# An encoder layer with attention and mLSTM heads: the dot products of the last eight modulation columns move from the way into the FFN to the mLSTM stage

## Chip, core and metric

The kernel runs on one core of a Trainium2 chip. The core has a matmul engine (PE, whose weight loads are counted apart as PEld), a vector engine (DVE), a scalar engine (ACT), a general engine (POOL) and a queue processor (SP), which here issues nearly all transfers between DRAM and the on-chip memory. Each engine works through its own instructions strictly in the order in which the program holds them; one that has to wait holds up all that stand behind it on that engine. This goes for SP too: a transfer that may not be issued yet holds back the transfers behind it. The metric is the device time of one execution in microseconds, lower is better, as the median of several runs.

## What is computed

One layer on 1024 tokens of width 1024, all in float32. A conditioning vector `c` is turned into six shift, scale and gate vectors (the modulation), and these steer two residual blocks:

```python
cond = jax.nn.silu(c)
mod = cond @ w_ada[l] + b_ada[l]
sh1, sc1, g1, sh2, sc2, g2 = jnp.split(mod, 6, axis=-1)
h = modulate(rms_norm(x, norm_mix_g[l]), sh1, sc1)
proj = h @ w_in[l]
...
y_attn = axial_gqa_attention(q_a, k_a, v_a, q_norm_g[l], k_norm_g[l], tables)
y_mem = bidirectional_mlstm(qk_m, v_m, o_m, gates, conv_w[l], conv_b[l], gate_b[l], mlstm_norm_g[l])
mix = jnp.concatenate([y_attn, y_mem], axis=-1) @ w_out[l]
x = x + g1[:, None, :] * mix
h = modulate(rms_norm(x, norm_ffn_g[l]), sh2, sc2)
ffn = (jax.nn.silu(h @ w_gate[l]) * (h @ w_up[l])) @ w_down[l]
x = x + g2[:, None, :] * ffn
return rms_norm(x, final_norm_g)
```

The modulation is a row of 6144 numbers, each the dot product of `silu(c)` with one column of `w_ada`. Held as 48 columns of 128 numbers, the last eight columns (40 to 47) are `g2`, the gate of the FFN. It is used only where the FFN's result is added to the residual, at the very end.

## The kernel before

Features lie on the 128 partitions and tokens along the free dimension, so a matrix of 1024 by 1024 is eight tiles of 128x1024, or sixteen halves of 128x512. Products of float32 are made from a high and a low part of each operand: three matmuls on PE for one product (`mm3`, lines 294 to 297, a "triple" below). ACT makes the high part of a weight (`whi`), POOL the low one (`wlo`).

**The order of instructions** is set by a planner that runs while the program is written out. A `Clock` keeps an expected time for every engine and every transfer and emits each instruction when its inputs are expected to be there. PE's work is a set of generators, the streams, of which the first that is ready goes on; `ck.need(flags)` moves the expected time on until the flags are set and emits, on the way, the pending work of the other engines, but nothing of a stream of PE. On the chip only the resulting order on each engine remains, and the waits.

**The stages.** (1) Norm, modulation columns 0 to 15, the start of the input projection; (2) attention, with more of the projection as filler for PE; (3) the mLSTM stage; (4) the way into the FFN; (5) gate and up products; (6) the down product and the final norm.

**The mLSTM stage (line 1922 on)** handles four heads, one after another, as four streams: `states` (transposes of k, lines 1675 and 1703, tiles `mk`, `wv`, `U`, `Cs`), `front` (scores, tiles `E`, `W`, `mq`), `back` (numerators, tiles `na`, `ni`, `num`) and `transposed`, which turns a half head's finished result `hs` (line 1848). `last` holds the steps from the numerators to `hs`, on DVE, POOL and ACT; there is one buffer each for `hs` and `so`, so the next half head can write `hs` only when PE has turned the former. PE's filler is first the rest of the input projection, `chunk_unit`: eight pieces `acct` per chunk, stored as `v_d` or `o_d` through `vstg`. When its last piece is done, the pool `big` and the projection's input are closed, the residual stream `x` is loaded into their place (16 transfers), and the filler becomes `out_unit`, the output projection: 12 matmuls into a tile `acc` (two buffers), which DVE adds to `x` with the gate `mod[:, 16 + f]`. Head 2's `mk` and `v` are loaded at about the same place.

**The way into the FFN (line 1958 on)** has the 16 output units of the mLSTM's half: DVE adds each to `x`, ACT squares it, DVE sums the squares (`ssq`), a matmul with ones (`ms`, line 1159) makes the mean square, ACT and DVE its root (`nv`, `ny`), and `norm2` scales all tiles of `x` by it and splits them (`h11*h`, `h11*l`) for the first FFN products.

**The modulation's later columns** are loaded in halves of 128x512 (`ada`, 256 KB each) by `ada_late`, 64 in all, two for each of the columns 16 to 47. One call issues at most one half, and only if the half `ahead` places earlier is expected to be done; DVE then multiplies it with `cond` and sums in the same instruction (SCALAR_TENSOR_TENSOR into `modacc`). Since the `ada` tiles are a ring of `ahead` buffers, SP may issue a half only when DVE has done with the one `ahead` before. In the kernel before, 48 halves run during the projection and the attention. The last 16 (the columns of `g2`) run on the way into the FFN, in a pool of their own with a ring of four, after `cond` has been loaded and put through silu a second time:

```python
adpool = tc.tile_pool(name="ad", bufs=1, side="right")
PP["ada"] = adpool.__enter__()
cond_ok = load_cond(PP["ada"])
ck.streams([un], stop=lambda: cond_ok.done and ada_late(64, 4))
while not summed:
    ck.need(*adas[-2:])
    ada_late(64, 4)
adpool.__exit__(None, None, None)
```

`ada_late` returns nothing, so the stop condition never holds: it only serves to call `ada_late` between two pieces of PE's work.

Of the kernel before, what the change touches and what calls it, by code (L numbers as in the profile page):

```python
# [18 lines left out]
DRAM = bass.MemoryType.DRAM  # L19
# [50 lines left out]
class Flag:  # L70
    """done: what sets it is emitted; t: when that is expected to end"""
# [12 lines left out]
class Engine:  # L84
    """An engine's instructions with their expected times."""
# [39 lines left out]
class Clock:  # L125
    """Emits instructions in the order of expected times (us), each engine's in the order in which they are ready."""
# [16 lines left out]
    def chain(self, delay, *steps, flag=None, bg=None):  # L143
        """Functions that follow one another. bg: the engine of each step; the step waits until that is idle."""
# [24 lines left out]
    def dma(self, nbytes, issue):  # L169
        """delay until a transfer that is issued now has arrived"""  # L170
        self.dma_q = max(self.dma_q, self.now) + issue
        self.dma_t = max(self.dma_t, self.dma_q + 0.65) + nbytes / 360e3
        return self.dma_t + DMA_LAT - self.now
# [6 lines left out]
    def need(self, *flags):  # L180
        """What sets the flags is emitted before what follows."""
        for f in flags:
            while not f.done:
                self.pop()
            self.until(f.t)
# [10 lines left out]
    def add_pe(self, dt):  # L196
        """work of the tensor engine that is not a stream's"""
        self.t += dt
# [6 lines left out]
    def streams(self, mains, fills=(), stop=None):  # L205
        """Runs streams, the first that is ready first, until the mains have ended or stop() holds."""
# [14 lines left out]
class Stream:  # L221
    """A part of the tensor engine's work: a generator that yields the flags that its next piece needs."""
# [15 lines left out]
def layer_kernel(ctx, tc, xT, c, w_ada, vecs, cons, rope, w_f, w_t0, w_t, w_o, w_gu, w_d, out):  # L238
# [8 lines left out]
    # ---------------------------------------------------------------- constants  # L247
# [23 lines left out]
    # DRAM scratch  # L271
# [39 lines left out]
    def psum_open(name, tags, bufs=1):  # L311
        """tags: name -> (tag, buffers)"""
# [7 lines left out]
    class slot:  # L320
        """what frees the next tile of a tag"""
# [26 lines left out]
    with tc.manual_schedule():  # L348
# [12 lines left out]
        def load_cond(pool):  # L361
            """silu of c, the same for all partitions"""
# [11 lines left out]
        # ---------------------------------------------------- weights in a ring of six pieces  # L374
# [46 lines left out]
        def raw(shape, src, flag, arrived):  # L421
            """a transfer into the ring of three; flag: it has been used; arrived(tile, delay)"""
# [10 lines left out]
        def split(p, delay, src, shape, *before, lo=None):  # L433
            """the parts of a piece"""
# [12 lines left out]
        def piece(i):  # L447
            """a piece; its transfer, where it has one of its own"""
# [11 lines left out]
        def load_piece():  # L460
            """the next piece, once there is room for it"""
# [17 lines left out]
        # ---------------------------------------------------- norm 1, modulation, first three tiles  # L479
# [13 lines left out]
        for k in range(KT):  # L493
            def sum_up(k=k):
                """adds a tile's squares"""
# [34 lines left out]
        def rstd_steps(ms, scale, tag, put, flag=None):  # L530
            """1/sqrt(scale*ms + eps), with one Newton step"""
# [25 lines left out]
        def h_steps(k):  # L557
            """the modulated norm of a tile and its parts"""
# [22 lines left out]
        def h_when(k):  # L581
            """starts a tile when its columns of the modulation are there"""
# [26 lines left out]
        # ---------------------------------------------------- q and k: gain, mean square, rotation  # L609
# [6 lines left out]
        def rope_steps(i, accs):  # L616
            """i: q tile 0..3, or 4 for k"""
# [77 lines left out]
        # ---------------------------------------------------- units of the projection  # L695
# [3 lines left out]
        def tile_mms(w0, last):  # L699
            """two halves of a tile of features; last(n, acc, flag) when half n is summed"""  # L700
# [26 lines left out]
        def conv_unit(i, w0):  # L727
# [19 lines left out]
            def silu():  # L747
                """2*silu(y) = y*(1 + tanh(y/2))"""
# [23 lines left out]
        def chunk_unit(ci, w0):  # L772
# [5 lines left out]
            for j in range(NJ):  # L778
                if ci == 3 and j >= 5 and OPL[0]:
                    load_y(0, 0)  # L780
# [28 lines left out]
        # ---------------------------------------------------- gate rows: fw heads at 0..3, bw heads at 32..35  # L809
        def gate_steps():  # L810
# [100 lines left out]
            def decay():  # L911
                # decay of a chunk: exp(rend + mprev), spread over all partitions
# [19 lines left out]
        def ada_late(last=48, ahead=2):  # L932
            """the next half of a column of the modulation that is not needed at once"""
# [11 lines left out]
        # ---------------------------------------------------- attention  # L945
# [16 lines left out]
        def scores():  # L962
            """scores and softmax of a tile of queries"""
# [30 lines left out]
        def turned():  # L994
            """weights transposed, four tiles of keys"""
# [43 lines left out]
        # ---------------------------------------------------- output projection of the attention  # L1039
# [64 lines left out]
        # ---------------------------------------------------- norms of x1 over all features  # L1104
# [7 lines left out]
        def new_x1(k, n, dt):  # L1112
            """a place of a half tile of the residual stream, for that or for a part of an operand"""
# [6 lines left out]
        def spill(n, k, flag):  # L1120
            """the residual stream to DRAM; its place on chip takes parts of the FFN's operands"""
# [7 lines left out]
        def root(ms, w, then):  # L1129
            """1/sqrt(ms/D + eps), with one Newton step"""  # L1130
# [11 lines left out]
        def square(n, k, flag, then):  # L1142
            """adds a tile's squares; after the last: the reciprocal root of the mean square, for then(n, root)"""
# [21 lines left out]
        # ---------------------------------------------------- FFN's input: quarters, and their sums (Winograd's form)  # L1165
# [51 lines left out]
        # ---------------------------------------------------- FFN, gate and up: seven products for a pair of tiles  # L1217
# [29 lines left out]
        def set_piece(e, p, i, m):  # L1247
            """an operand of a set: a quarter of the weights or a sum of quarters"""
# [812 lines left out]
```

## Time and profile before

| | |
|---|---|
| median of the runs | 1433.75 us |
| the three runs | 1430.2, 1433.75, 1435.06 us |
| span of the profiled execution | 1431.8 us (its own time is not listed apart from its span) |
| PE busy | 1310.1 us, 91% of the span |
| DVE, ACT, POOL busy | 1075.9, 660.6, 792.6 us |
| mLSTM stage: first transposes to the last chunk piece | 515 to 574 us |
| mLSTM heads 2 and 3 with output units | 575 to 667 us |
| the 16 last halves of `ada`: issue of the first, end of the last on DVE | 673.6 to 726.4 us |

Each row of a view gives a start, a length, the engine, the line of the program, the operation and the tiles (output<-inputs). Nearly all work of DVE, ACT and POOL has line 96, as one helper records it, so such rows are told apart by their tiles. In brackets stand the idle time of the engine ahead of the row and what ended it.

### The profile page before, as it was taken

The page shows a single profiled execution, that of the slowest core. Times are in us where ns is not written, and L with a number is a line of the kernel's source. Part 1 is how long each engine was busy: PE and PEld are TensorE (multiplying, and loading weights), DVE is VectorE, ACT ScalarE, POOL GpSimd, SP SyncE. Part 2 cuts the span into 40 slices and gives each one's busy share as a digit, 9 for nine tenths or more (in the row PEclk, how much of TensorE's full clock was granted, in tenths as well). Part 3 has the DMA queues.
Part 4 walks back from the last instruction along what each step waited for, and adds up shares of the span by engine and source line. Part 5 has one row for each costly group of instructions (what it writes and reads, how often), then busy time and mean ns, then how long its engine had stood idle before and what let it go on. Part 6 is the DMA issues. An engine that isn't in the chain of part 4 may idle for free.

```text
span 1431.8 us, 19550 instructions
## 1 busy us (share of the span) xinstructions
PE 1310.1 (91%) x6594; PEld 1075.7 (75%) x6602; DVE 1075.9 (75%) x1542; ACT 660.6 (46%) x1191; POOL 792.6 (55%) x624
## 2 busy tenths in 40 slices
PE   5789799999999999899877899999999999979997
PEld 2577677888878988777655688888888887757786
DVE  6947989987788836776899786766666654988676
ACT  5444326677666645454555333332333234433462
POOL 5555454444444336766557564554544444799942
PEclk9899899999999999999999999999999999999999
DMA  7446452322112144824742342232333159623324
GB/s 285 158 127 198 148 153 78 118 66 77 44 52 60 38 136 127 291 94 165 239 155 67 102 141 103 96 106 101 111 110 102 62 185 339 247 67 88 103 63 151
DMA packets 103172, 184.40 MB, mean 129 GB/s; under 512 B 11296, under 2 KB 32672, under 8 KB 103072
## 3 DMA queue, kind: packets, MB, share of 16 engines
q1 hardware_dynamic: 89968, 161.06, 35.2%
q10 hardware_dynamic: 13104, 22.10, 4.2%
q8 instruction: 52, 0.85, 0.3%
q14 instruction: 48, 0.39, 0.1%
HBM read 136.19 MB, written 43.25 MB: 125 GB/s over the span
## 4 chain that ended last, share of the span: by engine, by line
PE 55%; DVE 19%; issue 8%; DMA 7%; POOL 6%; ACT 3%; SPq 1%; DVEq 0%; POOLq 0%; ACTq 0%
PE acc L296 13%; PE acc L295 13%; PE acc L297 13%; POOL wlo L96 3%; DVE x L96 3%; DVE ada L96 3%; DVE sst L96 3%; PE av L1025 2%; DMA wst<-act_d 2%; PE T L1006 2%; DVE PT L96 2%; PE S L974 2%; DVE y L96 2%; PE acct L295 2%; PE acct L297 1%
## 5 line engine op out<-in xcount | busy, mean ns | idle before, releaser
L96 POOL TENSOR_TENSOR wlo<-wst,whi 128x512 fp32r<-128x512 f32 (+2 forms) x208 | 309.0, 1492 | 227.4 <-ACT whi L96 211.2
L96 ACT ACTIVATE whi<-wst 128x512 fp32r<-128x512 f32 (+2 forms) x219 | 131.9, 606 | 141.8 <-PE acc L297 22.4
L96 POOL TENSOR_SCALAR P<-P,sst 128x1024 f32<-128x1024 f32 x64 | 88.9, 1392 | 141.2 <-DVE sst L96 99.8
L296 PE MATMUL acc<-x,whi 128*128 128x512 f32 x352 | 139.6, 397 | 3.3 <-DVE x L96 3.3
L96 POOL TENSOR_TENSOR wlo<-wr,whi 128x512 fp32r<-128x512 f32 x60 | 83.5, 1392 | 78.3 <-ACT whi L96 74.9
L295 PE MATMUL acc<-hh,whi 128*128 128x512 f32 x224 | 97.8, 436 | 13.5 <-ACT hh L96 11.3
L297 PE MATMUL acc<-whi,wcl 128*128 128x512 f32 x244 | 98.1, 402 | 9.5 <-POOL wcl L96 9.5
L96 ACT ACTIVATE P<-S,sst,colq 128x1024 f32<-128x1024 f32 x64 | 77.3, 1207 | 52.2 <-DVE sst L96 47.8
L295 PE MATMUL acc<-whi,wch 128*128 128x512 f32 x244 | 96.8, 397 | 4.0 <-ACT wch L96 4.0
L296 PE MATMUL acc<-hl,whi 128*128 128x512 f32 x224 | 92.8, 414 | 8.2 <-POOL hl L96 4.5
L296 PE MATMUL acc<-wlo,wch 128*128 128x512 f32 x244 | 96.9, 397 | 1.1 <-POOL wlo L96 1.1
L297 PE MATMUL acc<-hh,wlo 128*128 128x512 f32 x224 | 91.5, 409 | 0.0
L96 DVE SCALAR_TENSOR_TENSOR ada<-ada,cond 128x512 f32<-128x512 f32 (+1 forms) x79 | 84.9, 1082 | 7.3 <-DMA ada<-in_w_ada_dram 7.2
L96 DVE TENSOR_TENSOR sg<-acc,sg 128x512 f32<-128x512 f32 x67 | 45.4, 687 | 59.3 <-PE acc L297 58.9
L96 ACT ACTIVATE PT<-T 128x512 fp32r<-128x512 f32 x128 | 71.4, 597 | 37.8 <-PE T L1006 37.1
L96 DVE TENSOR_TENSOR PT<-T,PT 128x512 fp32r<-128x512 f32 x128 | 82.8, 681 | 7.2 <-ACT PT L96 7.1
L96 ACT ACTIVATE whi<-wr 128x512 fp32r<-128x512 f32 x60 | 37.9, 632 | 106.1 <-DVE wr L96 49.6
L96 POOL TENSOR_TENSOR wlo<-s,whi 128x512 fp32r<-128x512 f32 x44 | 60.8, 1383 | 38.3 <-ACT whi L96 31.7
L295 PE MATMUL acct<-whi,hh 128*128 128x256 f32 (+1 forms) x256 | 79.3, 310 | 2.4 <-ACT xp L96 1.0
L296 PEld LDWEIGHTS acc<-x,whi 128*128 128x128 f32 x352 | 66.5, 189 | 19.2 <-DVE x L96 4.2
L96 DVE SCALAR_TENSOR_TENSOR x<-acc,mod,x 128x512 f32<-128x512 f32 (+1 forms) x92 | 62.7, 719 | 24.1 <-PE acc L297 24.1
L1006 PE MATMUL T<-con,P 128*128 128x128 f32 x512 | 70.2, 275 | 10.4 <-DVE PT L96 7.6
(457 smaller groups left out, 3875.1 us busy)
## 6 DMA issues: line engine op xcount, KB each, us to landing
wr<-in_w_gu_dram SPq DMA_DIRECT2D x66, 256.0 KB, 2.8
ada<-in_w_ada_dram SPq DMA_DIRECT2D x64, 256.0 KB, 3.6
wd<-in_w_d_dram SPq DMA_DIRECT2D x22, 512.0 KB, 7.0
wst<-in_w_gu_dram SPq DMA_DIRECT2D x34, 256.0 KB, 3.1
wst<-act_d SPq DMA_DIRECT2D x33, 256.0 KB, 4.1
ada<-in_w_ada_dram SPq DMA_DIRECT2D x16, 512.0 KB, 4.9
wst<-in_w_o_dram SPq DMA_DIRECT2D x32, 256.0 KB, 4.3
act_d<-sg ACTq DMA_DIRECT2D x31, 256.0 KB, 2.0
```

Of the source, the lines that this page charges most:

```text
L96: return fn(*args, **kw)
L295: nc.tensor.matmul(acc, w[0], x[0], start=first, stop=False)
L296: nc.tensor.matmul(acc, w[0], x[1], start=False, stop=False)
L297: nc.tensor.matmul(acc, w[1], x[0], start=False, stop=last)
L974: nc.tensor.matmul(sp[:, halves(n)], qs[:, j * P:(j + 1) * P], k2[g][m][:, halves(n)], start=m == 0, stop=m == 1)
L1006: nc.tensor.transpose(tp[:, k], Pt[q][:, (4 * b + k) * P:(4 * b + k + 1) * P], ident)
L1025: nc.tensor.matmul(av, va[:, k, h // 4], PT[it][m][:, k], start=(k, m) == (0, 0), stop=(k, m) == (NJ - 1, 1))
```

## The change

`chunk_unit` calls `ada_late(64)`, with the default ring of two, before each of its pieces once the mLSTM stage runs. `cond` is loaded and put through silu at the start of that stage, in the pool `big`, which also holds the `ada` ring. After the last chunk piece a loop brings in what is left and sums it, before `big` is closed; the extra pool and the loop on the way into the FFN are gone.

```diff
@@ chunk_unit
             for j in range(NJ):
+                if OPL[0]:
+                    ada_late(64)
                 if ci == 3 and j >= 5 and OPL[0]:
                     load_y(0, 0)
@@ start of the mLSTM stage
-        bp = big_open(3)
+        bp = PP["ada"] = big_open(3)
+        load_cond(bp)
...
         ck.streams(mem, [un], stop=lambda: un.wait is None and all(f.done for v in vo_ok for f in v))
+        while not summed:
+            ck.need(*adas[-2:])
+            ada_late(64)
         BIGP[0].__exit__(None, None, None)
@@ the way into the FFN
-        adpool = tc.tile_pool(name="ad", bufs=1, side="right")
-        PP["ada"] = adpool.__enter__()
-        cond_ok = load_cond(PP["ada"])
-        ck.streams([un], stop=lambda: cond_ok.done and ada_late(64, 4))
-        while not summed:
-            ck.need(*adas[-2:])
-            ada_late(64, 4)
-        adpool.__exit__(None, None, None)
+        ck.streams([un])
         opool.__exit__(None, None, None)
```

The rest of the diff removes comments.

How the instructions stand on the engines shows at three places. The first is SP at the end of the last chunk, before: `o_d<-vstg` stores the last chunk piece, `x_...<-in_xT` are loads of the residual stream, `mk` and `v_...` are head 2's operands.

```order
L300 DMA wst<-in_w_o_dram 128x512 x2
L300 DMA o_d_96<-vstg 128x256
L300 DMA x_5900<-in_xT_dram 128x512
L300 DMA mk<-mqk_d_91 128x1024
L300 DMA v_5906<-v_d_94 128x8x128
```

The same place of SP, now.

```order
L300 DMA o_d_96<-vstg 128x256
L300 DMA so<-o_d_95 128x4x128
L300 DMA ada<-in_w_ada_dram 128x512
L300 DMA ym_d_82<-ymt 128x512
L300 DMA wst<-in_w_o_dram 128x512
L300 DMA ada<-in_w_ada_dram 128x512 x6
L300 DMA mk<-mqk_d_91 128x1024
L300 DMA v_6002<-v_d_94 128x8x128
L300 DMA x_6015<-in_xT_dram 128x512
```

Nine halves have gone out beside the chunks. The tenth, a store of the mLSTM's result, a weight load and the last six halves now stand between the last store of a chunk and the loads of head 2 and of `x`.

The second place is DVE there, before: the rows around the first addition of an output unit to `x` (`x_5900`), among them the steps of head 1's second half (`dn` to `hs<-hs,ss`), and head 2's first `W` and `Cs`.

```order
L96 SCALAR_TENSOR_TENSOR x_5900<-acc,mod,x_5900 128x512
L96 SCALAR_TENSOR_TENSOR dn<-num 128x8
L96 TENSOR_TENSOR dn<-dn,cols 128x8
L96 RECIPROCAL dn<-dn 128x8
L96 TENSOR_TENSOR hs<-num,dn 128x512
L96 SCALAR_TENSOR_TENSOR x_5922<-acc,mod,x_5922 128x512
L96 TENSOR_TENSOR hs<-hs,hs_5931 128x512
L96 SCALAR_TENSOR_TENSOR W<-tr,W 128x256 x2
L96 TENSOR_REDUCE ss<-hs_5931 128x4
```

DVE now, from the same step of head 1 (`hs_5901` is its scratch tile, `x_6015` the first tile of `x`).

```order
L96 TENSOR_TENSOR hs<-num,dn 128x512
L96 TENSOR_TENSOR hs<-hs,hs_5901 128x512
L96 TENSOR_REDUCE ss<-hs_5901 128x4
L96 TENSOR_SCALAR ss<-ss 128x4
L96 SCALAR_TENSOR_TENSOR ada,modacc<-ada,cond 128x512
L96 TENSOR_TENSOR hs<-hs,ss 128x512
L96 SCALAR_TENSOR_TENSOR ada,modacc<-ada,cond 128x512 x6
L96 TENSOR_TENSOR mod<-modacc,vec 128x8
L96 TENSOR_TENSOR mod<-mod,modacc 128x8
L96 SCALAR_TENSOR_TENSOR x_6015<-acc,mod,x_6015 128x512
L96 SCALAR_TENSOR_TENSOR x_6022<-acc,mod,x_6022 128x512
L96 SCALAR_TENSOR_TENSOR W<-tr,W 128x256 x2
```

The additions to `x` and head 2's `W` no longer mix with head 1's steps: they stand behind all of these and behind the last halves. On PE, which waits for them, both half heads of head 1 are now turned right behind the last chunk piece (eight transposes `tr<-con,hs`), ahead of the output units, which before surrounded them; then come seven triples of output units, head 2's first `tr<-con,mk`, one more triple, and one that needs the first addition to `x`. On POOL the steps of head 1's second half (`hs`, `so`, `ss`, `hs` again) now stand behind or between four low parts of output weights (`wlo`).

The third place is DVE on the way into the FFN, before, from the end of the root on (`x_...<-x_...,ny` scales a tile of `x`).

```order
L96 SCALAR_TENSOR_TENSOR ny<-nv,ny 128x512
L96 TENSOR_TENSOR ssq<-ssq,sq 128x512
L96 SCALAR_TENSOR_TENSOR ada,modacc<-ada,cond 128x512
L96 TENSOR_TENSOR x_6037<-x_6037,ny 128x512
L96 SCALAR_TENSOR_TENSOR x_5944<-acc,mod,x_5944 128x512
L96 TENSOR_TENSOR x_6071<-x_6071,ny 128x512
L96 SCALAR_TENSOR_TENSOR ada,modacc<-ada,cond 128x512
L96 TENSOR_TENSOR x_6086<-x_6086,ny 128x512
L96 SCALAR_TENSOR_TENSOR ada,modacc<-ada,cond 128x512
```

The same place now (`x_6129` to `x_6222` are the tiles that were `x_6037` to `x_6136`).

```order
L96 SCALAR_TENSOR_TENSOR ny<-nv,ny 128x512
L96 TENSOR_TENSOR ssq<-ssq,sq 128x512
L96 TENSOR_TENSOR x_6129<-x_6129,ny 128x512
L96 SCALAR_TENSOR_TENSOR x_6030<-acc,mod,x_6030 128x512
L96 TENSOR_TENSOR x_6143<-x_6143,ny 128x512
L96 TENSOR_TENSOR x_6163<-x_6163,ny 128x512
L96 TENSOR_TENSOR x_6184<-x_6184,ny 128x512
```

The dot products are gone from between the scalings; the rest keeps its order.

## The prediction

> **What bounds the kernel now.** I read the busy times of stretches first, to see which engine fills which stage; then the waits of PE; then the rows around each place that the change touches. The columns of the first view are the stretch, its length, the busy time and count of PE, PEld, DVE, ACT and POOL, the granted TensorE clock, the busy share of the DMA engines, and GB/s.
>
> ```profile
> 535.00:555.00 20.00, 19.83 (x148) 18.63 (x148) 14.25 (x40) 12.28 (x36) 12.28 (x19) 1.00 0.42 126
> ...
> 575.00:601.50 26.50, 26.47 (x135) 21.41 (x134) 18.46 (x32) 14.46 (x37) 24.22 (x35) 1.00 0.97 336
> 601.50:620.00 18.50, 14.73 (x76) 12.87 (x79) 14.56 (x34) 7.53 (x21) 10.30 (x16) 0.91 0.40 131
> 620.00:640.00 20.00, 18.23 (x97) 14.59 (x96) 15.57 (x35) 10.00 (x28) 15.33 (x21) 1.00 0.22 73
> 640.00:660.00 20.00, 19.74 (x103) 16.36 (x103) 16.45 (x36) 9.35 (x23) 14.11 (x11) 1.00 0.42 138
> ...
> 691.00:735.00 44.00, 32.94 (x114) 24.07 (x113) 40.82 (x59) 23.19 (x38) 23.86 (x15) 0.85 0.62 197
> ```
>
> Beside the first heads (535 to 555) and with heads 2 and 3 (575 to 601.5, 640 to 660) PE is the bound: 19.83 of 20, 26.47 of 26.5, 19.74 of 20 us. On the way into the FFN it is DVE: 40.82 of 44 us, while PE stands for 11 us and runs at a mean clock of 0.85. So the change takes work from where DVE is the bound to where PE is, and there any new wait of PE is lost time.
>
> The waits of PE from 660 to 900 us (engine, waiting tile, what it waited for: us in all, times, longest) name three that DVE makes there:
>
> ```profile
> PE acc L296 <- DVE h113l L96: 4.7, 1, 4.7
> PE ms L1159 <- DVE ssq L96: 3.3, 1, 3.3
> PE acc L296 <- DVE h111l L96: 2.3, 1, 2.3
> ```
>
> **What is removed on the way into the FFN.** Sixteen dot products leave DVE. In two stretches, for the tile `ada` alone (busy time of DVE first):
>
> ```profile
> 691.00:703.00 12.00, 5.30 (x10) 0.00 (x0) 0.00 (x0) 0.72 0.71 238
> ...
> 703.00:728.50 25.50, 8.71 (x14) 0.00 (x0) 0.00 (x0) 1.00 0.52 156
> ```
>
> The first stretch matters little:
>
> ```profile
> 691.57 0.39 PE L297 MATMUL acc<-yah,wlo 128*128 128x512 f32 x1
> ...
> 692.85 0.74 DVE L96 SCALAR_TENSOR_TENSOR x<-acc,mod,x 128x512 f32<-128x512 f32 x1
> ```
>
> The last addition to `x` of the first eight units waited behind a dot product, from 692.0, when PE was done with the unit, to 692.85: 0.8 us of the 3.3 us wait goes. The other dot products there ran while DVE would have waited anyway, for ACT's square and for the root. The second stretch is a closed queue from `ny` to `h113l`:
>
> ```profile
> 703.32 0.69 DVE L96 SCALAR_TENSOR_TENSOR ny<-nv,ny 128x512 f32<-128x512 f32 x1
> ...
> 704.53 1.78 DVE L96 SCALAR_TENSOR_TENSOR ada<-ada,cond 128x512 f32<-128x512 f32 x1
> ...
> 725.01 1.34 DVE L96 SCALAR_TENSOR_TENSOR ada<-ada,cond 128x512 f32<-128x512 f32 x1
> ...
> 728.88 0.68 DVE L96 TENSOR_TENSOR h113l<-x,h113h 128x512 fp32r<-128x512 f32 x1
> ```
>
> Seven dot products, 704.53 the first and 725.01 the last, take 8.7 us (the row above). Without them and 0.8 us earlier, `h113l` starts at 728.9 - 8.7 - 0.8 = 719.4. PE comes to it after its output units. In the next rows it starts `h113h` at 724.53, after the 2.3 us wait for `h111l`, so without both it gets there at 724.5 - 2.3 - 0.8 = 721.4, and `h113l` is there at 720.1. Both waits go: 2.3 + 4.7 = 7.0 us.
>
> ```profile
> 724.30 0.39 PE L297 MATMUL acc<-h112h,wlo 128*128 128x512 f32 x1
> 724.53 0.40 PE L295 MATMUL acc<-h113h,whi 128*128 128x512 f32 x1
> 729.62 0.79 PE L296 MATMUL acc<-h113l,whi 128*128 128x512 f32 x1 [4.69 <-DVE h113l L96]
> 730.21 0.63 PE L297 MATMUL acc<-h113h,wlo 128*128 128x512 f32 x1
> ...
> 734.48 0.63 PE L295 MATMUL acc<-h113h,whi 128*128 128x512 f32 x1
> ```
>
> After that wait PE runs slower, 0.63 us a matmul where it was 0.40. From 730.21 to 734.48 are ten steps of 0.427 us, where full-speed rows (724.30, 724.53) are 0.23 apart: 1.9 us, with the first and the last about 2.5. **The gain is 7.0 + 0.8 + 2.5 = 10.3 us.** Its bounds: 7 us, if the slow clock stays; and 14.0 us, all the dot products after 691 (5.30 + 8.71), if DVE, which is full again later, passes on each of them:
>
> ```profile
> 780.00:790.00 10.00, 4.92 (x19) 3.41 (x19) 10.00 (x10) 3.35 (x7) 7.07 (x5) 0.99 0.41 128
> ...
> 739.36 0.69 DVE L96 TENSOR_SCALAR nv<-ms 128x512 f32<-128x512 f32 x1 [2.20 <-ACT ny L96]
> ```
>
> I take 10.3, since DVE waits 2.2 us for the second root ahead of 739.36, by which its queue is used up: what PE loses up to there is what can come back. The DMA traffic of the sixteen halves goes too (4 MB); no wait of PE there names a transfer.
>
> **What is added beside the first heads.** Ten halves of the sixteen run there, by the order in front. A dot product takes, by the rows of `ada` over the whole span (shortest, median, longest in ns, so the halves set the median):
>
> ```profile
> L96 DVE SCALAR_TENSOR_TENSOR ada<-ada,cond x79: 654/691/2877, 22.2 to 725.0; 128x512 f32<-128x512 f32 x64, 128x1024 f32<-128x1024 f32 x15
> ```
>
> Ten times 0.69 are 6.9 us, in a stretch where DVE is busy 14.25 of 20 us: there is room, but each stands in DVE's order ahead of a `Cs` or `num` that PE soon needs, and holds DVE if its transfer is late. Between nothing and 6.9 us I take 1.5, nearer to nothing, because PE holds chunk pieces between most of its waits there.
>
> At the start of the stage come a load of `cond`, its silu and two ACT table loads, one to silu's and one back to the exponential's:
>
> ```profile
> 673.88 1.28 ACT L96 ACT_TABLE_LOAD   x1
> ```
>
> The load of `cond` can go out while SP waits for the last store of the attention. The table load back stands ahead of head 0's first `W`. Between nothing and 2.6 us I take 1.0.
>
> **What is added behind the last chunk.** Six halves are left there, and nothing of PE's work was emitted between them. I count from T, the end of the last chunk piece. SP now issues, in this order: the last `o_d`, `so`, half ten, `ym_d`, a weight load, six halves, head 2's `mk` and `v`, `x`. The times from issue to landing:
>
> ```profile
> wr<-in_w_gu_dram SPq DMA_DIRECT2D x66, 256.0 KB, 2.8
> ada<-in_w_ada_dram SPq DMA_DIRECT2D x64, 256.0 KB, 3.6
> ...
> mk<-mqk_d SPq DMA_DIRECT2D x4, 512.0 KB, 4.5
> ```
>
> Two things hold PE. First, it has to turn head 1's second half before any output unit. That half's `hs` needs the single buffer that PE frees by turning the first half, at T + 0.6. From there POOL is the slow engine; its rows of before for the same work:
>
> ```profile
> 579.77 1.29 POOL L96 TENSOR_TENSOR wlo<-wst,whi 128x512 fp32r<-128x512 f32 x1
> 581.40 1.05 POOL L96 TENSOR_TENSOR hs<-num,dn 128x512 f32<-128x512 f32 x1 [0.34 <-DVE dn L96]
> ...
> 587.40 1.02 POOL L96 TENSOR_TENSOR ss<-ss,both 128x4 f32<-128x4 f32 x1
> ...
> 590.25 0.62 POOL L96 TENSOR_SCALAR so<-so 128x512 f32<-128x512 f32 x1
> ...
> 593.50 1.29 POOL L96 TENSOR_TENSOR hs<-hs,so 128x512 f32<-128x512 f32 x1
> ```
>
> Four `wlo` stand among them now: 4 x 1.29 + 1.05 + 0.62 + 1.02 + 1.29 = 9.1 us, from T + 1.1 (after ACT's `vstg` and `whi`) to T + 10.2. PE idles from T + 0.6 to there: 9.6 us. Then it turns the half and runs seven triples of 0.70 us (three steps of 0.23), to T + 15.7.
>
> Second, `mk`. Half ten is multiplied at T + 6.5, ahead of DVE's `hs<-hs,ss`. The ring has two buffers, so of the last six halves the second, fourth and sixth follow half ten, each 3.6 + 0.7 + 0.1 = 4.4 us after the one before: multiplied at 10.9, 15.3 and 19.7. SP may issue the sixth at T + 15.4 and `mk` at T + 15.8, which lands at T + 20.3. PE idles from 15.7 to 20.3: 4.6 us. Then it waits for the first addition to `x`, which stands behind the sixth half on DVE and whose transfer left two places behind `mk`: 1.0 us more. **The loss is 9.6 + 4.6 + 1.0 = 15.2 us**, since before PE had no idle time at all from 575 to 601.5; its own first `tr<-con,mk` came 7.9 us after the chunk's end, with `mk` issued right behind the last store:
>
> ```profile
> 573.93 0.28 PE L297 MATMUL acct<-whi,hl 128*128 128x256 f32 x1
> ...
> 574.97 0.33 SPq L300 DMA_DIRECT2D o_d<-vstg  x1
> 575.35 0.42 SPq L300 DMA_DIRECT2D x<-in_xT_dram  x1
> 575.82 0.45 SPq L300 DMA_DIRECT2D mk<-mqk_d  x1
> ...
> 582.10 0.38 PE L1675 MATMUL tr<-con,mk 128*128 128x128 f32 x2
> ```
>
> Below: if the weights don't stand in POOL's way and the halves land in 2.8 us (the row of `wr`, the same size), 11 us. Above: if they land in 4.7 us, the median (second number) of the halves on the way into the FFN, 19 us.
>
> ```profile
> DMA to landing us min/median/max: 2.5/4.7/7.1
> ```
>
> A rule of the Trainium skill speaks for the change: "DMA: Bandwidth & Descriptors", Rules for kernel authors, says to overlap a transfer with compute by issuing it early and waiting for it late, so that its fixed setup cost is hidden. By the rule none of the landings would count and the last six would cost nothing; by the rows six of the sixteen can't be issued early, because the ring holds two. What the rule gives is the first rival.
>
> **The sum.** 15.2 + 1.5 + 1.0 - 10.3 = +7.4 us on the span of 1431.8, so 1439.2. The median of the three runs stands 1.95 us above that span, which I keep: **1441.2 us**, 0.5% slower. (About 0.3%, 4.3 us, is what a measurement of this kernel can tell from no change.) From the bounds: loss 11 + 0 + 0 to 19 + 6.9 + 2.6, gain 14.0 to 7, so -3 to +21.5 us, 1430.8 to 1455.3.
>
> **Rivals.**
> - *The transfers are hidden.* The last six halves land while PE has the seven triples and head 1's turns, and head 2's loads are not late. For it: DVE and SP have room there, and the halves are only 1.5 MB. Against it: the six are two deep and stand ahead of `mk` on SP. Then only the start costs 1.0 us: 1433.75 - 10.3 + 1.0 = 1424.5. It decides once the loss is under 10.3 - 4.3 = 6 us. Chance 0.12.
> - *The stall is there but is made good.* PE waits for DVE in heads 2 and 3 as well (from 601.5 to 640 it is busy 33.0 of 38.5 us, by two stretches of the same view), and if head 2's chain then runs with less in its way, or the gain nears 14, the two cancel: 11 + 1.5 + 1.0 - 14.0 = -0.5, 1433.3. Chance 0.14.
> - *The first heads are slowed as well.* Each dot product beside them holds DVE for its transfer, and SP, waiting for a buffer, holds the loads of `mq`. With 6.9 in place of 1.5 and the loss at its upper end: 19 + 6.9 + 2.6 - 10.3 = 18.2, 1452. Chance 0.10.
>
> **How the numbers follow.** My forecast, slower by 4.3 to 16 us (1438 to 1450), has 0.64. Slower in all: 0.64 + 0.10 = 0.74; within 0.3%: 0.14; faster: 0.12. The range from 1431 to 1450 leaves out the first rival and most of the third, 0.2 together.
>
> **What would show it.** Right: a group `tr<-con,hs` of eight whose second half waits some 9 us for POOL's `hs`; a wait of some 5 us of `tr<-con,mk` for its transfer; six `ada` on DVE about 2 us apart with waits for DMA between them; `mk` issued some 16 us after the last `o_d`; and behind it the waits for `h111l` and `h113l` gone, with 7 to 14 us less from `ms` to the second `ms`. Wrong: `mk` on chip within 8 us of the last chunk piece, or the `h113l` wait still there for another reason, such as POOL's halves of the same split.

## The result, and the profile after

The changed kernel takes **1443.54 us** (median of 4 runs, 1442.86 to 1445.63), the kernel before 1432.85 (4 runs beside it, 1430.2 to 1435.06): ratio 1.0064, 95% interval 1.0041 to 1.0088. It is slower. The profiled run took 1442.86 us, its span 1441.1 us, 9.3 us more than before.

The waits of TensorE (PE) in the changed kernel from 500 to 900 us (engine, waiting tile, what it waited for: us in all, times, longest):

```profile
PE tr L1850 <- POOL hs L96: 11.9, 2, 11.4
PE ms L1161 <- DVE ssq L96: 6.4, 2, 5.6
...
PE acc L295 <- DVE x L96: 3.7, 2, 2.8
...
PE tr L1677 <- DMA mk<-mqk_d: 1.9, 1, 1.9
```

The waits for `h111l` and `h113l` are gone (the one for `ssq` has grown from 3.3 to 6.4 us, as PE now comes to the second one sooner), and three new ones stand there: for `hs`, `mk` and `x`. Where they lie, by PE's instructions in order of time (start, duration, what it is; in brackets the idle time before it and what ended it):

```profile
579.72 0.28 PE L297 MATMUL acct<-whi,hl 128*128 128x256 f32 x1
580.51 0.66 PE L1850 MATMUL tr<-con,hs 128*128 128x128 f32 x4 [0.51 <-POOL hs L96]
592.60 1.12 PE L1850 MATMUL tr<-con,hs 128*128 128x128 f32 x4 [11.43 <-POOL hs L96]
593.37 0.78 PE L295 MATMUL acc<-yah,whi 128*128 128x512 f32 x1
593.94 0.63 PE L296 MATMUL acc<-yal,whi 128*128 128x512 f32 x1
...
601.42 0.42 PE L1677 MATMUL tr<-con,mk 128*128 128x128 f32 x2 [1.90 <-DMA mk<-mqk_d]
...
605.34 0.80 PE L295 MATMUL acc<-yah,whi 128*128 128x512 f32 x1 [2.80 <-DVE x L96]
...
713.86 1.12 PE L1161 MATMUL ms<-ssq,ones 128*128 128x512 f32 x2 [0.80 <-DVE ssq L96]
745.12 2.08 PE L1161 MATMUL ms<-ssq,ones 128*128 128x512 f32 x2 [5.62 <-DVE ssq L96]
```

The last chunk piece ends at T = 580.0. Behind it PE stands for 0.51 + 11.43 + 1.90 + 2.80 = 16.6 us. SyncE's (SP's) DMA queue in the same stretch:

```profile
580.50 0.33 SPq L300 DMA_DIRECT2D o_d<-vstg  x1
...
582.91 13.87 SPq L300 DMA_DIRECT2D ada<-in_w_ada_dram  x6
596.82 0.42 SPq L300 DMA_DIRECT2D mk<-mqk_d  x1
```

Six halves hold SP for 13.87 us, since each waits for one of two buffers; `mk` goes out 16.3 us after the last `o_d`. Busy times by stretch, with the columns of the prediction's first view:

```profile
535.00:555.00 20.00, 20.00 (x150) 18.75 (x148) 15.51 (x46) 12.22 (x36) 11.15 (x15) 1.00 0.49 145
...
579.90:607.50 27.60, 10.96 (x41) 7.93 (x41) 14.73 (x26) 5.48 (x10) 14.20 (x21) 0.72 0.64 215
...
709.60:753.60 44.00, 37.58 (x149) 28.64 (x148) 37.52 (x40) 26.94 (x45) 26.37 (x18) 0.92 0.54 173
```

Beside the first heads PE is as full as before (20.00 of 20 us). Behind the last chunk it works 10.96 of 27.6 us at a mean clock of 0.72. On the way into the FFN (the third row stands as far ahead of and behind the first `ms` as 691 to 735 did before) it works 37.58 of 44 us where it worked 32.94, at 0.92 for 0.85. The kernel before had its sums of squares at

```profile
695.26 2.08 PE L1159 MATMUL ms<-ssq,ones 128*128 128x512 f32 x2 [3.30 <-DVE ssq L96]
...
737.58 1.02 PE L1159 MATMUL ms<-ssq,ones 128*128 128x512 f32 x2
```

so 42.3 us lay between them, and 31.3 lie there now: 11.1 us are won. The first one comes 18.6 us later than before, though.

### The profile page after: what moved, and what is told of

Its sections match the earlier page's. It is cut to its first block, busy times and chain, and to the rows that moved or that the text cites. A ratio compares the mean times of both kernels' runs of the same rounds, so it can differ in the third digit from the quotient of the medians.

```text
span 1441.1 us, 19548 instructions
## 1 busy us (share of the span) xinstructions
PE 1310.1 (91%) x6602; PEld 1078.2 (75%) x6602; DVE 1083.1 (75%) x1542; ACT 661.0 (46%) x1192; POOL 792.0 (55%) x624
## 4 chain that ended last, share of the span: by engine, by line
PE 52%; DVE 21%; issue 7%; POOL 7%; DMA 7%; ACT 5%; SPq 1%; ACTq 0%; DVEq 0%; POOLq 0%
PE acc L296 12%; PE acc L295 12%; PE acc L297 12%; DVE x L96 4%; DVE ada L96 3%; POOL wlo L96 3%; PE av L1027 2%; DVE sst L96 2%; PE T L1008 2%; DVE y L96 2%; PE S L976 2%; DVE PT L96 2%; DMA qd<-q_d 2%; PE acct L295 1%; PE acct L297 1%
## 5 line engine op out<-in xcount | busy, mean ns | idle before, releaser
L96 POOL TENSOR_TENSOR wlo<-wst,whi 128x512 fp32r<-128x512 f32 (+2 forms) x208 | 304.0, 1467 | 219.9 <-ACT whi L96 206.3
L295 PE MATMUL acc<-hh,whi 128*128 128x512 f32 x224 | 97.3, 435 | 13.4 <-ACT hh L96 11.1
L96 DVE SCALAR_TENSOR_TENSOR ada<-ada,cond 128x512 f32<-128x512 f32 (+1 forms) x79 | 80.4, 1025 | 22.8 <-DMA ada<-in_w_ada_dram 22.5
L296 PEld LDWEIGHTS acc<-x,whi 128*128 128x128 f32 x352 | 66.6, 189 | 16.7 <-DVE x L96 1.6
```

The lines of the kernel that those rows point to most:

```text
L96: return fn(*args, **kw)
L295: nc.tensor.matmul(acc, w[0], x[0], start=first, stop=False)
L296: nc.tensor.matmul(acc, w[0], x[1], start=False, stop=False)
```

## The experiments

Kernels that were timed together ran on one chip and shared the runs of the kernel before, so each row has the median of before beside it; rows with different medians of before are compared by their ratios. The last column is read from each trace: from the end of the last chunk piece (the last `acct` row) to the start of the first `ms`. The change has no part in that stretch but its halves and what they shift. (For the kernel before it is 121.1 us, but there, as in e1, some 2.6 us of head 1's products run behind the last chunk that the other kernels run ahead of it.) It is from one execution each, and those of e3 and e9 took 4.5 and 5.5 us longer than their medians. The runs that leave dot products out also set `modacc` to zero at the start.

| run | dot products | us (before) | ratio, 95% | chunk end to `ms` |
|---|---|---|---|---|
| e1 | none | 1424.06 (1435.41) | 0.9908, 0.9883–0.9933 | 121.6 |
| e2 | 9 beside chunks | 1426.14 (1435.41) | 0.9929, 0.9909–0.9950 | 117.0 |
| e3 | 9, stretch without PE work | 1433.50 (1435.41) | 0.9985, 0.9970–1.0001 | 125.4 |
| e4 | 9 + 7 beside heads 2, 3 | 1438.33 (1435.41) | 1.0019, 1.0004–1.0034 | 127.8 |
| e5 | 9 + 7 behind the store, no transfers | 1436.88 (1435.16) | 1.0013, 0.9999–1.0027 | 127.2 |
| e6 | e3, low parts on DVE | 1434.38 (1435.16) | 0.9993, 0.9978–1.0008 | 124.4 |
| e7 | change, `mk`, `v` ahead of the 7 | 1440.60 (1435.16) | 1.0046, 1.0029–1.0064 | 130.5 |
| e8 | 16 beside chunks, ring of four | **1427.01** (1435.16) | 0.9952, 0.9933–0.9971 | 118.1 |
| e9 | e3, units ahead of the turn | 1437.58 (1433.23) | 1.0027, 1.0008–1.0046 | 127.9 |
| e10 | change, units ahead of the turn | 1447.73 (1433.23) | 1.0090, 1.0067–1.0112 | 138.7 |
| e11 | 9 + 7 on the way into the FFN | 1431.60 (1433.23) | 0.9985, 0.9967–1.0003 | 117.6 |
| e12 | e4 without its 7 | 1435.19 (1434.98) | 0.9996, 0.9978–1.0014 | 126.6 |
| change | 9 + 7 behind the store | 1443.54 (1432.85) | 1.0064, 1.0041–1.0088 | 133.9 |

**e1, e2: the gain alone, and the nine beside the chunks.**

```diff
 e2:     bp = PP["ada"] = big_open(3)
         load_cond(bp)
 ...
-        while not summed:
-            ck.need(*adas[-2:])
-            ada_late(64)
+        mod_sum(40, 48)
 e1, besides: no call of ada_late(64) in chunk_unit, no load_cond(bp)
```

> The change without the last sixteen dot products at all: neither the nine beside the chunks, nor the seven behind the last store, nor the second load of the condition (the modulation's columns 40 to 47 are left out and hold only their bias). What is left is the gain on the way into the FFN. Theory: the time before less 10.3 to 11.2 us (the working's gain, and what the changed trace shows between the two sums of squares), 1421.5 to 1422.5 us. Rival, by which the new way into the FFN is bound by something other than the dot products (POOL's halves of the split, the square roots): less than 6 us come back, 1427 or more.

> The change with the nine halves beside the last chunks and the load of the condition, but without the seven behind the last store (those seven dot products are left out). Theory: the nine cost little, 2.5 us (the working's 1.5 for the first heads and 1.0 for the start) to 3.2 us (by how much the last chunk piece ends later in the changed trace, less the head 1 work that now stands ahead of it) above the run without any, 1424 to 1426 us. Rival, by which the first heads carry the loss: each of the nine holds DVE for its transfer, 7 us or more above the run without any, over 1429, and the seven add little.

Without any dot product the kernel is 11.4 us faster by the medians (13 by the ratio); with the nine 9.3 us. So the gain is there, and the nine with the load of the condition cost some 2 us of it, which the intervals don't tell from nothing. In the run with nine hardly anything holds PE behind the last chunk (0.5 us for `hs`, and behind `mk` 1.6 us for `x`):

```profile
579.83 0.28 PE L298 MATMUL acct<-whi,hl 128*128 128x256 f32 x1
...
588.39 0.38 PE L1678 MATMUL tr<-con,mk 128*128 128x128 f32 x2
...
697.12 1.13 PE L1162 MATMUL ms<-ssq,ones 128*128 128x512 f32 x2 [0.48 <-DVE ssq L96]
```

Its `mk` is turned 8.3 us after the chunk's end (before: 7.9). So the loss is with the last seven.

**e3: the planner's stretch without the seven.** While the loop runs, the planner's clock moves on 30.2 us and nothing of PE's streams is written out.

```diff
-        while not summed:
-            ck.need(*adas[-2:])
-            ada_late(64)
+        ck.until(ck.t + 30.2)
+        mod_sum(40, 48)
```

> The change with the nine halves, and in place of the seven only the planner's stretch of 30.2 us in which nothing of TensorE's work is written out (the seven dot products are left out, and their transfers too). It keeps the order in which the engines get head 1's end, and takes the transfers from SP and the dot products from DVE. Theory (two causes, the order on POOL and the transfers on SP): PE still waits 9 to 12 us for POOL's hs in head 1's second half, but no longer for mk and x; of the 18 us between the run with nine and the changed kernel, about half comes: 1432 to 1436 us. Rival A, all of it is the order: 1441 to 1444. Rival B, all of it is the transfers in front of mk: 1424 to 1427, with no wait for hs over 3 us.

```profile
595.14 1.12 PE L1851 MATMUL tr<-con,hs 128*128 128x128 f32 x4 [10.76 <-POOL hs L96]
...
602.49 0.38 PE L1678 MATMUL tr<-con,mk 128*128 128x128 f32 x2
```

The theory's number came: 7.4 us above e2, with the wait for `hs` whole and those for `mk` and `x` gone. The changed kernel, 1.0064 x 1435.41 = 1444.6 on this chip, stands another 11 us above (8.5 by the last column). Two causes, neither of them small.

**e6, e9: what in the stretch costs.** First the weights' low parts are taken from POOL:

```diff
-                (lo or gps).tensor_sub(p[1], src(), p[0].bitcast(F32))
+                (lo or LO[0] or gps).tensor_sub(p[1], src(), p[0].bitcast(F32))
 ...
+        LO[0] = dve
         ck.until(ck.t + 30.2)
+        LO[0] = None
```

> The run with the stretch alone (the seven dot products left out), with the low parts of the four output weights that are written out in that stretch made by DVE in place of POOL. Theory (the working's first term: POOL's queue is what PE waits for): 4 x 1.26 = 5 us of POOL's work go, the wait for hs falls from 10.8 to 5 to 7 us, and the time from 1433.5 to 1427 to 1430. Rival: the wait is the chain of head 1's end itself (DVE, ACT and POOL in turn), with the weights in POOL's own idle time: the wait stays at 9 us or more and the time over 1431.5.

The theory fell. The wait went from 10.76 to 9.41 us, and the time not at all. DVE, ACT and POOL in that run:

```profile
585.12 0.68 DVE L96 TENSOR_TENSOR hs<-hs,hs 128x512 f32<-128x512 f32 x1
...
588.59 0.63 ACT L96 ACTIVATE whi<-wst 128x512 fp32r<-128x512 f32 x1 [1.61 <-DMA wst<-in_w_o_dram]
589.25 0.69 DVE L96 TENSOR_TENSOR wlo<-wst,whi 128x512 fp32r<-128x512 f32 x1 [1.47 <-ACT whi L96]
589.86 0.68 DVE L96 TENSOR_TENSOR hs<-hs,ss 128x512 f32<-128x512 f32 x1
...
590.69 1.26 POOL L96 TENSOR_TENSOR hs<-hs,so 128x512 f32<-128x512 f32 x1 [1.81 <-DVE mod L96]
```

With no weight left on POOL, POOL waits (1.81 us) for DVE, and DVE waited for a weight whose transfer was late. So the run doesn't take the weights out of the chain's way altogether: on DVE the low parts at 582.45, 584.51 and 589.25 put its next steps off by 0.4, 0.6 and 0.7 us. Estimated from these rows, the chain without any weights would still hold PE for some 8 of the 10.8 us. Head 1's end is a chain over DVE, POOL and ACT that is long by itself. In the kernel before it took longer still, from this row to POOL's last `hs` (593.50 to 594.79, in the prediction's rows), 15 us, and PE was busy all along:

```profile
579.73 0.16 DVE L96 SCALAR_TENSOR_TENSOR dn<-num 128x8 f32<-128x8 f32 x1
```

What the stretch takes away is PE's work beside the chain. So the next run gives it some, 9 us of output units ahead of the second turn:

```diff
+        t0 = ck.t
+        ck.streams([un], stop=lambda: ck.t > t0 + 9.0)
         ck.streams(mem, [un])
```

> The run with the stretch alone (1433.5 us; the seven dot products left out), with 9 us of the output units written out ahead of the second turn of head 1. The engines' work for head 1's end is the same. The run with the low parts on DVE took the weights out of POOL's queue and PE still waited 9.4 us for hs, so that head 1's end is slow by itself, and what is missing is work for PE beside it. Theory: with fourteen triples (0.70 us each, 9.8 us) between the two turns the wait for hs falls under 3 us and the time to 1425 to 1429, near the run with nine (1426.1). Rival: the units that are put there are missing as cover beside heads 2 and 3, which then wait as much longer: 1431 or more.

The rival held. PE's waits from 500 to 900 us:

```profile
PE acc L296 <- ACT yah L96: 6.5, 1, 6.5
PE acc L296 <- DVE x L96: 5.8, 2, 4.9
...
PE tr L1851 <- POOL hs L96: 2.2, 2, 1.6
```

The wait for `hs` is nearly gone, one for `x` comes at once (4.85 us, ahead of 593.88), and one for `yah` behind the last turn of head 3 (ahead of 680.88), where the units are now missing. The time became 4 to 6 us worse than e3's (by the medians and by the ratios). Head 2's first `mk` is turned 8.3 us after the chunk's end in e2, 19.3 in e3 and 26.3 in e9. That this later start is what the stretch costs fits these rows, but no run shows it by itself; moving units about changes the name of the wait and doesn't bring the time back.

**e5, e7, e10: the seven transfers.** First the seven dot products without their transfers (each takes again the half that is on chip), then the two loads of head 2 ahead of the seven, then the units of e9 in the changed kernel itself.

```diff
 e5:
+            if n >= 57:
+                t, arrive = still[0], ck.dma(P * HALF * 4, 0.5)
 e7:
+        ck.need(*heads[0]["back"])
+        load_head(2)
         while not summed:
 ...
-            load_head(h)
+            if h != 2:
+                load_head(h)
```

> The changed kernel, but the last seven dot products run again on the half that is on chip already, so that their seven transfers (1.75 MB) are left out (seven sums come out other than they should); the planner's stretch and the seven instructions on DVE stay. The run with the stretch alone took 1433.5 us, and the changed kernel would take 1444.6 on that chip by its ratio of 1.0064. Theory: of those 11 us nearly all are the transfers, that is mk, v and x behind them on SP and the dot products waiting for them; seven dot products that wait for nothing are 4.9 us on a DVE that is idle there: 1432 to 1437 us, mk issued within 7 us of the last o_d, no wait for x over 1 us. Rival: it is DVE's time, with head 1's end and the additions to x behind the dot products: 1440 or more.

> The changed kernel, all sixteen dot products, but mk and v of head 2 are issued ahead of the seven halves (as before the change, right behind the last store) instead of behind them. Theory: the place of these two loads on SP is half or more of the 11 us between the stretch alone (1433.5) and the changed kernel (1444.6 on that chip): 1435 to 1439.5 us, no wait of PE for mk. Rival: the seven dot products themselves, with the first additions to x behind them, carry it: 1441 or more, and PE waits for x 4 us or more where it waited for mk.

> The changed kernel, all sixteen dot products, with the same 9 us of output units ahead of the second turn of head 1. Theory: the order alone doesn't mend it, since the units need their additions to x, and these stand on DVE behind the seven dot products with their transfers; there are two accumulators, so after two units (5.6 us) PE waits for x instead of hs, 8 us or more: 1438 to 1445. Rival: the wait for hs was most of the loss, and PE gets over it here: 1434 or less.

Without the transfers (e5) 3.4 us are left above e3 (4 by the ratios), hardly more than the intervals, so the transfers carry some 7 of the 11; the wait for `hs` is the same 11.43 us as in the changed kernel. With `mk` and `v` first (e7) PE waits for neither, and the time comes down only by about 4 us (1444.3 by the ratio on that chip, to 1440.6): a third of the 11 where half or more was expected, and just above the range. PE still waits 9.71 us for `hs`, and the wait for `mk` has moved to the next thing behind the seven. In e7, PE and DVE:

```profile
601.08 1.23 PE L1785 MATMUL na<-v,W 128*128 128x130 f32 x4 [4.38 <-DVE W L96]
...
599.71 0.69 DVE L96 SCALAR_TENSOR_TENSOR ada<-ada,cond 128x512 f32<-128x512 f32 x1 [1.13 <-DMA ada<-in_w_ada_dram]
...
600.61 0.75 DVE L96 SCALAR_TENSOR_TENSOR W<-tr,W 128x256 f32<-128x256 f32 x2
```

What PE gives to this `W` (`tr<-mq,mk`, started at 592.76, 1.05 us) was done at 593.8; it stands behind the last dot product on DVE, which waits for its half. With the units ahead (e10) the mechanism is the expected one, larger than I put it (1447.73 for at most 1445): two units run, then PE stands 15 us for the addition behind the seven:

```profile
602.26 0.77 PE L295 MATMUL acc<-yah,whi 128*128 128x512 f32 x1 [14.98 <-DVE x L96]
```

**e4, e12, e11, e8: other places for the seven.**

```diff
 e4, after the x loads of heads 2 and 3 (e12: the load alone):
+        adpool = tc.tile_pool(name="ad", bufs=1, side="right")
+        PP["ada"] = adpool.__enter__()
+        cond_ok = load_cond(PP["ada"])
-        ck.streams(mem, [un])
+        ck.streams(mem, [un], stop=lambda: cond_ok.done and ada_late(64, 1))
 e11: no loop; the pool "ad", load_cond and ada_late(64, 4) of before on the way into the FFN
 e8:
-                    ada_late(64)
+                    ada_late(64, 4)
+                    ada_late(64, 4)
 ...
-            ada_late(64)
+            ada_late(64, 4)
```

> All sixteen dot products: nine beside the last chunks as in the change, and the other seven beside heads 2 and 3, one at a time, with a load of the condition of their own, and no stretch without TensorE's work. Theory: what costs is where the seven stand, not that they run; one half of 0.7 us every 5 us or more fits on DVE beside heads 2 and 3, so 0 to 4 us above the run with nine, 1424 to 1430, faster than both kernels. Rival: heads 2 and 3 have no room either (PE busy there 19.7 of 20 us in places), and each of the seven delays PE by its 0.7 us and its transfer: 1433 or more.

> The run with nine halves beside the chunks and, at the start of heads 2 and 3, the load of the condition and its silu, but none of the seven dot products there (they are left out). The run with both (seven dot products one at a time beside heads 2 and 3) came out at 1438.3 us where 1424 to 1430 was expected, the run with neither at 1426.1. Its trace shows head 2's first na about 4.5 us later against the last chunk piece, with PE waiting 2.4 us for ACT's silu and two table loads of 1.28 us, and 6.4 us more between there and the first sum of squares. Theory: the condition costs 4 to 6 us and the seven dot products the rest: 1430 to 1432. Rival A: all of it is the condition, whose place shifts the order behind it: 1436 or more. Rival B: all of it is the dot products: 1428 or less.

> All sixteen dot products: nine beside the last chunks as in the change, the other seven on the way into the FFN as before the change, four at a time, with a load of the condition there, and no planner's stretch. Theory: the gain of 11 us belongs to the dot products in the closed queue of DVE between the two sums of squares (seven of them ran there before); seven of sixteen go partly where DVE waits anyway, so 2 to 6 us of the gain are lost: 1428 to 1432 us, on or under the time before. Rival: any dot product there costs its share, or the load of the condition and its silu set the end: 1434 or more.

> All sixteen dot products beside the last chunks: a ring of four halves in place of two, and two halves asked for at each chunk piece, so that none is left for behind the last store. Theory: nine cost 2.1 us there (1426.1 against 1424.1), so sixteen cost 3.7: 1427.8 us (1425.5 to 1430.5), faster than both kernels, with no stall behind the last chunk beyond what the run with nine has. Rival: the room beside the first heads is used up by nine, and the seven more cost their 0.7 us and part of their landing each, 6 us or more above the run with nine: 1432 or more.

e4 missed: 12 us above e2. By e12, some 9 of them are the second load of the condition and some 3 the seven dot products (e4 and e12 have intervals that overlap), so e12 came out above its theory's range too, by 3 us, and close under the rival that gave all of it to the condition. ACT and PE in e12:

```profile
586.76 1.28 ACT L96 ACT_TABLE_LOAD   x1 [1.95 <-DMA cond<-in_c_dram]
588.05 1.06 ACT L96 ACTIVATE cond<-cond 128x1024 f32<-128x1024 f32 x1
...
594.18 1.28 ACT L96 ACT_TABLE_LOAD   x1
...
589.11 0.47 PE L296 MATMUL acc<-yah,whi 128*128 128x512 f32 x1 [2.81 <-ACT cond L96]
```

ACT waits for the condition and then works on it 2.3 us while output units need ACT; the table comes back just ahead of head 2's first `W`. PE's direct wait is 2.8 us, `mk` is turned 13.6 us after the chunk's end (8.3 in e2), and PE's wait for `yah` behind heads 2 and 3 is 4.3 us (0.9 in e2); how this adds up to 9 was not taken further apart. e11 came out in its range. By the ratios it is 8 us above e2, but its trace shows only 2 of them behind the chunk's end (0.6 us in the last column, 1.9 between the sums of squares, and 0.6 back behind them); the rest lies ahead, where the two kernels are alike. So seven dot products on the way into the FFN, with the load of the condition there, cost some 2 us by the traces, and up to 8 can't be excluded.

e8 is **the version to keep**: 0.9952 of the time before, faster than both kernels, with all sixteen dot products done by 572.2 and `mk` again right behind the last `o_d`. The tile `ada` in its trace (instructions, shortest, median and longest ns, first and last start), and SP's queue:

```profile
L300 SPq DMA_DIRECT2D ada<-in_w_ada_dram x16: 376/432/847, 514.3 to 558.0; - x16
L96 DVE SCALAR_TENSOR_TENSOR ada<-ada,cond x16: 642/682/877, 520.1 to 571.5; 128x512 f32<-128x512 f32 x16
```

```profile
580.25 0.38 SPq L300 DMA_DIRECT2D o_d<-vstg  x1
580.69 0.44 SPq L300 DMA_DIRECT2D mk<-mqk_d  x1
```

The seven more cost 0.9 us over e2 by the medians, 3.3 by the ratios with intervals that overlap: less than their 4.9 us on DVE either way. Beside the first heads there was room for all sixteen.

e8 changes two things at once, the depth of the ring and the number of requests, and by the planner both are needed. The changed kernel has ten chunk pieces left in that stretch and asks once at each; nine halves went out, and one request was turned away since by the planner's times the ring was not free. Written out with the ring of four alone, the program has ten halves there: there are no more requests. With two requests per piece and the ring of two it has ten as well, since the ring turns both away at five of the ten pieces. Neither of these two was timed.

## Why the prediction was right, and which terms were off

The forecast was slower, 1441.2 us in a range of 1431 to 1450; 1443.5 came, by the forecast mechanism.

- **The gain, 10.3 us.** 11.4 by e1 and 11.1 between the two sums of squares. Both waits on the split parts went. The bounds 7 and 14.0 held.
- **Beside the first heads and the start, 2.5 us.** 2.1 by e2 against e1, for nine halves where the working counted ten; the intervals are wider than that.
- **The first stall, 9.6 us.** Right in kind, order and nearly size: 11.4. Its working named POOL's queue with four weights as the cause, and that step holds only in part. POOL is busy 10.3 of the first 12 us behind T, but e6 took the weights out of its queue and 9.4 us stayed, some 8 by the estimate above without any. The sum of POOL's steps came near because the chain over DVE, ACT and POOL is nearly as long, which is luck. What it left out shows in DVE's rows of the changed kernel:

```profile
583.81 1.74 DVE L96 TENSOR_TENSOR hs<-hs,hs 128x512 f32<-128x512 f32 x1 [0.94 <-POOL hs L96]
...
589.08 1.74 DVE L96 TENSOR_TENSOR hs<-hs,ss 128x512 f32<-128x512 f32 x1 [0.90 <-POOL ss L96]
```

  These two take 0.68 us each in e6, so 2.1 us are time behind POOL, which has `wlo` at those moments in the changed kernel and none in e6. The Trainium skill, "SBUF — State Buffer", Who interferes with whom, says that a VectorE instruction with two SBUF inputs contends with a GpSimd instruction that reads SBUF; the trace agrees.
- **The wait for `mk`, 4.6 us.** 1.9. The transfer was judged well (`mk` issued 16.3 us after the last `o_d` for about 16; PE could go on at T + 21.4 for T + 20.3), but PE came to it later, held by the first stall. The two together are 13.3 us for a forecast of 14.2.
- **The first addition to `x`, 1.0 us.** 2.8: mis-sized. Its transfer left SP at 597.93 and it ran at 604.53, 6.6 us later; DVE, done with the halves, waited for it:

```profile
597.93 0.60 SPq L300 DMA_DIRECT2D x<-in_xT_dram  x1
...
604.53 0.75 DVE L96 SCALAR_TENSOR_TENSOR x<-acc,mod,x 128x512 f32<-128x512 f32 x1 [3.81 <-DMA x<-in_xT_dram]
```

- **Not counted: the clock after a stall.** The prediction credited the slow clock to the gain and didn't charge it to the new stalls. Behind the first one the matmuls 593.94 to 595.2 take 0.63 us and stand 0.43 apart, where full-speed rows stand 0.23 apart; it comes again behind the wait for `x`. From the chunk's end to the first `ms` PE is busy 110.6 us, and 107.8 in e2 with the same work: 2.8 us, most of which this would be.
- **The net.** Head 2's first `na` comes 24.9 us later than before (610.94 for 586.03) and the first `ms` 18.6 us later, so the way between them is 6.3 us shorter. That looks like the second rival, by which heads 2 and 3 make the stall good, but it isn't shown: 2.5 of the 6.3 us are the shorter wait ahead of the first `ms` (3.30 to 0.80), and in e2, where hardly anything stalls, `na` to `ms` is as short (101.8 us; 102.9 in the changed kernel, 109.2 before). Against e2, which has the same chunks, the first `ms` comes 16.7 us later (16.9 from the chunk's end: PE stands 14.1 us longer and is busy the 2.8). With the 2.1 for the nine and the gain of 11.4 that makes 7.4 us, as the working's sum has it: the stalls cost 1.5 us more than put, the nine 0.4 less, and the gain was 1.1 larger. At the second `ms` it is 7.5 us over the kernel before; another 1.8 were lost behind it (span +9.3), which no run explains.
- **The rival in which transfers are hidden** needed them to be issued early. The working held that six of the sixteen can't be, because the ring holds two; by the planner one request per piece stands in the way as well. e8 lifts both, and there the rival holds: 1427.0 for its 1424.5. The rival in which the first heads are slowed too is out by e2.

## What to carry over

Background work that misses its window is not just late: left for a place where one engine's queue must take it all at once, it stands ahead of everything that queue still has to issue. Ask first how often it is asked for, and how deep its ring must be, to finish inside the window; here two more buffers of 2 KB per partition together with two halves asked for at a time were worth 1.1% (1.0064 against 0.9952), 16 us.

When a wait has been taken away and the time stays, look for the next instruction behind the same transfers (`mk`, then `W`, then `x`): the wait's name moves, and what they all stand behind stays. And work that fills one gap is missing in the next.

## What the runs showed of the hardware

The condition's second load with its silu and two table loads (1.28 us each) takes 3.6 us of ACT. The run with it at the start of head 2 was 9 us slower (e12 against e2, which ran on another chip; 9.6 by the ratios), its place in the order included. At the start of the chunks, together with nine dot products, it cost some 2 us (e2 against e1). The slow clock came after shorter waits too: behind one of 2.80 us, with 1.1 us of work between it and one of 1.90, the granted clock was 0.50 from 605.3 to 609.0, and the first matmul there took 0.80 us.
